# Output weights split two heads earlier and kept in DRAM, the first output projection woven into the last sweeps

## The chip, the cores and the metric

One core of a Trainium2 chip runs one launch of the kernel. The metric is the device time of that core in microseconds (us); the median of the runs of the kernel before is 2640.04 us. Engines are called as the profile calls them: PE (TensorE's matmuls), DVE (VectorE), ACT (ScalarE), POOL (GpSimd) and SP (SyncE, which here only issues DMAs).

## The reference

A block of a transformer-like network on one sequence of 2048 tokens with 1024 features. The part around the change:

```
hx = rmsnorm(x) * (1 + sc1) + sh1                        # modulated by a conditioning vector
heads = 4 HGRN2 heads and 4 retention heads on hx @ w_in # each a scan forward and a scan backward
mix_x = concat(normalised, gated heads)                  # 2048 x 1024
x = x + g1 * (mix_x @ w_out)                             # the output projection
hx2 = rmsnorm(x, norm2_g) * (1 + sc2) + sh2
x = x + g2 * conv_ffn(hx2)                               # up, 3-tap convolution, silu, down
return rmsnorm(x, final_g)
```

All inputs and outputs are 32-bit floats. The scales g1, sc2, sh2 and so on are pieces of silu(c) @ w_mod + b_mod.

## The kernel before

**Numbers.** Big products are made with pairs of 16-bit floats: a block is scaled by a power of two, rounded to f16, and the rest is kept as a second f16. `mm3` (L98) then takes three matmuls, high times high, high times low and low times high, into one accumulator. For the projections of the heads and the feed-forward part a seven-product scheme is used (`unit`, L550); the output projection is plain: 8 blocks k of 128 rows.

**Stages.** `run` (L1830) calls `setup`, `heads`, `out_proj`, `ffn_up` and `ffn_down`. Tokens are in four groups of 512 (`NG`), features in eight blocks of 128 (`KT`).

**Heads.** `heads` (L1027) walks over 32 steps s: head h = 0 to 7 (0 to 3 HGRN2, 4 to 7 retention) and i = 0 to 3 inside it, which takes the groups from the last to the first. A step (`step`, L1002) runs the backward sweep of head h on one group (`ret_sweep1`, L1246: scores times a decay table rA at L1254, transposes, state updates at L1274) and the forward sweep of head h - 1 on group i (`ret_sweep2`, L1281: states at L953, sum at L1286, the sum of squares on ACT at L963, a reciprocal root in small DVE steps at L79 to L90; and `ret_sweep2b`, L1289: scaling and gating at L1293, a transpose otp on PE at L970, a copy m on ACT at L1296 and a store to mixd in DRAM). `weave` (L991) mixes into it, piece by piece, the projection of the next step (`ret_proj`, L1201), which reads the normalised features hx from DRAM through ten tiles (L518, `RING`). Behind step 31 come four steps with only the last head's forward sweeps (L1107); the last head's gates (`ret_gate`, L1191) are the filler of step 31 and of the first two of these.

**Work spread by ticks.** Each step calls `tick` (L325) twice. A tick runs the second half of what it loaded last time, and loads the next n items of a list: weights of the next head (`head_weights`, L709), rows of the modulation (`mod_later`, L294), and in the last head the output weights. `out_weights` (L1311) gives eight items. The load puts 128 rows of w_out into one of two raw tiles (wor, L1323). The second half multiplies by g1 (L1332, DVE), squares and sums (L1334, ACT), adds up over partitions (a small matmul, L124), makes a power of two (`pow2`, L105, five small DVE steps), notes it in so (L1336, L1337), and scales and splits both halves into wo (L1342 on ACT, L1343 on DVE). The wo tiles lie in the slots q and z and stay in SBUF until the projection has used them. For the first block g1 is first spread over the partitions (`broadcast_cols`, L1300, into the slot FG).

**Output projection.** `mixed_pairs(g)` (L1347) finds the group's scale smk (L1361) from the eight values in so and a bound on the gates, then loads mixd block by block (mxf, L1376) and makes pairs mp of it (L1377 on ACT, L1378 on DVE). `out_product(g)` (L1389) takes four tiles of 128 tokens in two halves of 512 columns: 8 x 3 matmuls opp each, then x is added (L1404), squares are summed (L1405), x1 is stored to DRAM and scaled for the second norm (L1408). Its accumulators have the tag pj with three banks. `out_proj` (L1463) puts these together with the second norm (`second_norm_a`, `second_norm_b`), whose tiles y0 to y13 are in a pool that opens only when the head phase's pools are closed.

**What sets the order.** The program's order is the order in which these functions emit. A compile-time scheduler (L1888) then orders each engine's queue by a simulated timeline, so an instruction can be pulled ahead of others that were emitted earlier; each engine, SP too, works off its queue in order. `issue_after(ins)` (used at L312) keeps what is emitted inside it behind the instruction `ins` on its engine; `self.mark` is the last rA or state update of the backward sweep.

## Time and profile before

| | us |
|---|---|
| median of 3 runs | 2640.04 (2639.76 to 2642.2) |
| profiled execution, first to last instruction | 2636.4 |
| what lies around the span, against the median | 3.6 |
| PE busy | 2515.8 (95%) |
| DVE busy | 1887.8 (72%) |
| ACT busy | 1349.2 (51%) |
| POOL busy | 425.2 (16%) |

The profile gives no wall time of its own for the profiled execution, so its span stands in the table beside the median. Times in the profile's answers are counted from the span's first instruction. A line such as `L1332 DVE TENSOR_TENSOR wor<-wor,g1b` names the line of the kernel, the engine, the operation, and the written and read tiles; a bracket such as `[1.67 <-DMA ...]` is the idle time of that engine just before, and what ended it. PEclk is the clock granted to TensorE as a share of the full one. Matmul ends are modelled, so that a busy PE isn't always at its peak.

### The profile page before, as it was taken

How to read it: one execution, taken by the hardware profiler on the slowest of the kernel's cores; microseconds unless marked ns; L12 is line 12 of the kernel's file. 1: busy time of each engine (PE TensorE's matmuls, PEld its weight loads, DVE VectorE, ACT ScalarE, POOL GpSimd, SP SyncE). 2: the span in 40 equal slices, each digit the busy share in tenths (PEclk: the TensorE clock that was granted, in tenths of full speed). 3: DMA queues.
4: the chain of work that ended last, by engine and by line, in shares of the span. 5: the costliest groups of instructions: out<-in, count | busy, mean ns of one | idle time of the engine just before them, and what ended most of it. 6: DMA issues, size and time to landing. Idle time of an engine off the chain costs nothing. (4 is left out here: it accounts for less than half of the span.)

```text
span 2636.4 us, 56190 instructions
## 1 busy us (share of the span) xinstructions
PE 2515.8 (95%) x22763; PEld 1656.9 (63%) x22763; DVE 1887.8 (72%) x4275; ACT 1349.2 (51%) x2877; POOL 425.2 (16%) x409
## 2 busy tenths in 40 slices
PE   6799998999999999988998999999999999999998
PEld 3678887889899999984454444444444444444443
DVE  4888686786878778675558778888888887323656
ACT  5886466564654454453556556565555555211220
POOL 1100000000000000000354334343434433000000
PEclk7999999999999999998999999999999999999999
DMA  8324342441548567555421332333233236544552
GB/s 295 121 95 162 124 142 85 135 152 67 177 161 291 210 210 255 189 198 192 143 81 41 116 106 99 112 107 110 101 116 120 96 113 225 206 165 159 210 206 87
DMA packets 213621, 393.97 MB, mean 149 GB/s; under 512 B 15600, under 2 KB 97748, under 8 KB 208753
## 3 DMA queue, kind: packets, MB, share of 16 engines
q1 hardware_dynamic: 203808, 373.42, 40.8%
q10 hardware_dynamic: 9248, 16.79, 1.9%
q8 instruction: 178, 2.92, 0.5%
q14 instruction: 83, 0.67, 0.1%
q0 software_dynamic: 304, 0.17, 0.0%
HBM read 298.57 MB, written 91.75 MB: 148 GB/s over the span
## 5 line engine op out<-in xcount | busy, mean ns | idle before, releaser
L101 PE MATMUL pa<-feat,w 128*128 128x512 f16 x704 | 265.0, 381 | 7.6 <-ACT ta L592 5.6
L102 PE MATMUL pa<-feat,w 128*128 128x512 f16 x704 | 267.9, 381 | 0.0
L103 PE MATMUL pa<-feat,w 128*128 128x512 f16 x704 | 267.3, 380 | 0.0
L102 PE MATMUL pd<-wd,actl 128*128 128x512 f16 x616 | 233.3, 379 | 0.0
L103 PE MATMUL pd<-wd,actl 128*128 128x512 f16 x616 | 233.3, 379 | 0.0
L101 PE MATMUL pd<-wd,actl 128*128 128x512 f16 x616 | 232.6, 379 | 0.0
L102 PEld LDWEIGHTS <-w 128*128 128x128 f16 x1232 | 120.9, 98 | 150.9 <-issue 13.0
L103 PEld LDWEIGHTS <-w 128*128 128x128 f16 x1232 | 121.0, 98 | 147.0 <-issue 3.2
L101 PEld LDWEIGHTS <-w 128*128 128x128 f16 x1232 | 120.9, 98 | 141.9 <-issue 3.1
L102 PEld LDWEIGHTS <-hx 128*128 128x128 f16 x1824 | 179.4, 98 | 7.7 <-issue 5.9
L1407 POOL TENSOR_TENSOR ssq<-ssq 128x1 f32<-128x1 f32 x16 | 4.7, 292 | 1102.8 <-ACT junk L1405 1102.8
L101 PEld LDWEIGHTS <-hx 128*128 128x128 f16 x1824 | 179.9, 99 | 2.2
L103 PEld LDWEIGHTS <-hx 128*128 128x128 f16 x1824 | 179.6, 99 | 0.9
L1642 ACT ACTIVATE st<-act,modT 128x512 f16<-128x512 f32 x154 | 107.4, 717 | 109.6 <-DVE act L1632 64.1
L1643 DVE SCALAR_TENSOR_TENSOR st<-act,modT,st 128x512 f16<-128x512 f32 x154 | 140.3, 946 | 29.7 <-ACT st L1642 28.8
L101 PE MATMUL pa<-w_vg,hx 128*128 128x128 f16 x800 | 141.8, 219 | 1.1 <-ACT ct L592 0.7
L102 PE MATMUL pa<-w_vg,hx 128*128 128x128 f16 x800 | 141.7, 219 | 0.0
L103 PE MATMUL pa<-w_vg,hx 128*128 128x128 f16 x800 | 141.7, 219 | 0.0
L101 PE MATMUL pc<-feat,w 128*128 128x512 f16 x352 | 134.8, 383 | 2.2 <-ACT feat L1417 1.3
L103 PE MATMUL pc<-feat,w 128*128 128x512 f16 x352 | 135.2, 384 | 0.0
L102 PE MATMUL pc<-feat,w 128*128 128x512 f16 x352 | 135.0, 383 | 0.1
L101 PE MATMUL pa<-hx,w_z 128*128 128x256 f16 x464 | 127.0, 274 | 1.6 <-DVE K L634 1.3
(552 smaller groups left out, 7357.3 us busy)
## 6 DMA issues: line engine op xcount, KB each, us to landing
hx<-hxd SPq DMA_DIRECT2D x212, 512.0 KB, 4.7
actd<-st SPq DMA_DIRECT2D x154, 256.0 KB, 2.0
actl<-actd SPq DMA_DIRECT2D x28, 1024.0 KB, 5.0
wur<-in_w_up_dram SPq DMA_DIRECT2D x44, 512.0 KB, 3.8
raw<-in_w_in_dram SPq DMA_DIRECT2D x36, 512.0 KB, 4.7
wm<-in_w_mod_dram SPq DMA_DIRECT2D x64, 256.0 KB, 3.7
hxd<-hx SPq DMA_DIRECT2D x28, 512.0 KB, 3.9
wdb<-in_w_down_dram SPq DMA_DIRECT2D x44, 256.0 KB, 3.8
```

What stands on the lines that cost most here:

```text
L101: mm(ps, lhs(0), rhs(0), start=start, stop=False, skip_group_check=True)
L102: mm(ps, lhs(0), rhs(1), start=False, stop=False, skip_group_check=True)
L103: mm(ps, lhs(1), rhs(0), start=False, stop=stop, skip_group_check=True)
L1407: nc.gpsimd.tensor_tensor(ssq[:, 0:1], ssq[:, 0:1], ssq[:, 1:2], ALU.add)
L1642: nc.scalar.activation(p[:, 0], v, AF.Copy, scale=s)
L1643: nc.vector.scalar_tensor_tensor(p[:, 1], v, s, p[:, 0], ALU.mult, ALU.subtract)
```

## The change

The output weights' items get three parts (load, square, split) and are spread over ticks from head 6 on, in the gaps behind head 7's weights and the last modulation rows; the list may now run on into head 7, so the loop that empties it ahead of a head's last step is left out for head 6. The multiply by g1 is put behind `self.mark`. Split weights are written to DRAM (wod) and read back, all of them, ahead of head 7's last step (`out_loads`); in between they use only q. `mixed_pairs` is parted into the scales (`mixed_scales`) and the pairs (`mixed_some`), and the output product is made a generator (`out_steps`), one half tile a piece. The four last steps now make group 0's scales and pairs, three half tiles of group 0's product as filler in each of the third and fourth, the second modulation, and group 1's scales and pairs 2 to 7. Group 1 sums its blocks in the order 2 to 7, 0, 1, with pairs 0 and 1 in y0. The fourth x1 tile of group 0 is two half tiles in z instead of y6. The rest of `out_proj` is as it was.

```diff
+        self.wod = [dp.tile([P, 2, 2, 512], F16, name=f"wod{k}") for k in range(KT)]
...
     def tick(self, n=2):
 
-        for comp in self.loaded:
+        later = []
+        for comp, *rest in self.loaded:
             comp()
+            if rest:
+                later.append(rest)
         now, self.todo = self.todo[:n], self.todo[n:]
-        for load, _ in now:
+        for load, *comps in now:
             if load:
                 load()
-        self.loaded = [c for _, c in now]
+            later.append(comps)
+        self.loaded = later
...
+                elif h < 2 * NH - 1:
+                    n = 5
+                    mods = self.mod_later(10) + self.mod_later(11)
+                    outs = self.out_weights()
+                    ticks = [items[:1] + mods[:2], items[1:4] + mods[2:4], items[4:] + mods[4:6], mods[6:] + outs[:1]]
+                    ticks += [[o] for o in outs[1:]]
+                    items = [it for t in ticks for it in t + [none] * (n - len(t))]
                 else:
-                    items = self.out_weights()
-                    self.todo += items[:5]
-                    n = 1
+                    n, items = self.n_tick, []
+                self.todo += items
                 self.n_tick = n
             if i == NG - 1:
-                while self.todo or self.loaded:
-                    self.tick(4)
+                while h != 2 * NH - 2 and (self.todo or self.loaded):
+                    self.tick(self.n_tick)
                 if h == 2 * NH - 1:
-                    self.todo += items[5:]
+                    self.out_loads()
...
+        self.x0 = []
+        first = self.out_steps(0, self.x0)
         for i in range(NG):
-            self.weave(self.step(2 * NH, i, None, None, prev, None), self.ret_gate(NH - 1, i + 2, W, prev) if i < 2 else None, 3, 4)
-            if i == 1:
-                self.mixed_pairs(0)
+            if i == 0:
+                self.mixed_scales(0)
+                self.mixed_some(0, ((0, 1), (2, 3), (4, 5), (6,)))
+                filler, n = self.ret_gate(NH - 1, 2, W, prev), 4
+            elif i == 1:
+                self.mixed_some(0, ((7,),))
+                filler, n = self.ret_gate(NH - 1, 3, W, prev), 4
+            else:
+                if i == 2:
+                    self.mod2 = self.modulation(self.cp, self.kp, self.sv[:, V_N2:V_N2 + 8], self.modT[:, 0, 32:40],
+                                                self.modT[:, 0, 24:32], 1, 4.0)
+                else:
+                    self.mixed_scales(1)
+                    self.mixed_some(1, ((2, 3), (4, 5), (6, 7)))
+                filler, n = islice(first, 3), 3
+            self.weave(self.step(2 * NH, i, None, None, prev, None), filler, 3, n)
+        self.first = first
...
-            def comp():
+            def square():
...
-                w = self.wo[k] = [self.slot_tile([P, 2, 512], F16, "q" if 2 * k + half < 4 else "z", "wo") for half in range(2)]
+                w = raws[k, 1] = self.slot_tile([P, 2, 512], F16, "q", "wos")
                 raw = raws[k]
-                nc.vector.tensor_tensor(raw, raw, self.g1b, ALU.mult)
...
+                with self.tc.issue_after(self.mark.ins):
+                    nc.vector.tensor_tensor(raw, raw, self.g1b, ALU.mult)
+                nc.scalar.activation(w.rearrange("p a n -> p (a n)"), raw, AF.Square, scale=gain(k), accum_out=self.q8[:, k:k + 1])
+
+            def split():
+                raw, w = raws.pop(k), [self.slot_tile([P, 2, 512], F16, "q", "wos"), raws.pop((k, 1))]
+                s, i = self.pow2(self.wp, self.allsum(self.q8[:, k:k + 1]), 1, "w")
...
                     nc.scalar.activation(w[half][:, 0], v, AF.Copy, scale=rk)
                     nc.vector.scalar_tensor_tensor(w[half][:, 1], v, rk, w[half][:, 0], ALU.mult, ALU.subtract)
-            return load, comp
+                    nc.sync.dma_start(self.wod[k][:, half], w[half])
+            return load, square, split
...
+    def out_loads(self):
+
+        for k in range(KT):
+            self.wo[k] = [self.slot_tile([P, 2, 512], F16, "q" if k < 2 else "z", "wo") for half in range(2)]
+            for half in range(2):
+                self.nc.sync.dma_start(self.wo[k][half], self.wod[k][:, half])
...
-            mp = [self.slot_tile([P, 1, 2, G], F16, "z" if k < 2 else "vg", "mp") for k in range(KT)]
+            mp = [None] * 2 + [self.slot_tile([P, 1, 2, G], F16, "vg", "mp") for k in range(2, KT)]
...
+    def mixed_some(self, g, parts):
+
+        nc = self.nc
+        dst, _, smk, mp = self.mixp[g]
+        if mp[0] is None and parts[0][0] == 0:
+            w = self.slot_tile([P, 2, 2, G], F16, "y0", "mp")
+            mp[:2] = w[:, :1], w[:, 1:]
+        for ks in parts:
+            f = self.wp.tile([P, len(ks), G], F32, tag="wr", bufs=WR, name="mxf")
+            for kk, k in enumerate(ks):
                 nc.sync.dma_start(f[:, kk], self.mixd[k][:, g * G:(g + 1) * G])
                 nc.scalar.activation(dst(k)[:, 0], f[:, kk], AF.Copy, scale=smk[:, k:k + 1])
                 nc.vector.scalar_tensor_tensor(dst(k)[:, 1], f[:, kk], smk[:, k:k + 1], dst(k)[:, 0], ALU.mult, ALU.subtract)
...
+    def out_steps(self, g, x1):
+        order = (2, 3, 4, 5, 6, 7, 0, 1) if g == 1 else range(KT)
...
+                for j, k in enumerate(order):
+                    self.mm3(pp, lambda q: mp(k)[:, q, ts], lambda q: wo[k][half][:, q], j == 0, j == KT - 1)
...
     def out_proj(self):
-        self.mod2 = self.modulation(self.cp, self.kp, self.sv[:, V_N2:V_N2 + 8], self.modT[:, 0, 32:40],
-                                    self.modT[:, 0, 24:32], 1, 4.0)
         self.feats = [None, None]
-        x0 = self.out_product(0)
-        self.mixed_pairs(1)
+        x0 = self.x0
+        self.mixed_some(1, ((0, 1),))
+        for _ in self.first:
+            pass
         self.mixed_pairs(2)
```

More of the change, by code (lines that the diff above doesn't have):

```diff
@@ L1 @@
 from contextlib import ExitStack, nullcontext
-from itertools import chain
+from itertools import chain, islice
 import numpy as np
@@ L1371, in mixed_pairs @@
         dst = lambda k: mp[k // n][:, k % n]
-        for k0 in range(0, KT, 2):
-            f = self.wp.tile([P, 2, G], F32, tag="wr", bufs=WR, name="mxf")
-            for kk in range(2):
-                k = k0 + kk
+        self.mixp[g] = dst, io, smk, mp
+    def mixed_some(self, g, parts):
[7 more added lines that the diff above has]
+            for kk, k in enumerate(ks):
                 nc.sync.dma_start(f[:, kk], self.mixd[k][:, g * G:(g + 1) * G])
@@ L1397, in out_product @@
             ts = slice(i * P, (i + 1) * P)
             ssq = self.kp.tile([P, 2], F32, tag="ssq", bufs=2, name="ssq2")
[L1399 to L1400 removed]
+            for half, xh in enumerate(halves):
                 pp = self.ps("pj", [P, 512], "opp")
[L1402 to L1405 removed]
@@ L1411, in modulated, with out_product @@
+            yield
+    def out_product(self, g):
+        x1 = []
+        for _ in self.out_steps(g, x1):
+            pass
+        return x1
     def modulated(self, f, k, xn):
```

67 lines of the change are left out of this document (34 added, 33 removed).

## The prediction, blind

> **What bounds the kernel now.** First the page of the profile, for the whole execution.
>
> ```profile
> span 2636.4 us, 56190 instructions
> ...
> PE 2515.8 (95%) x22763; PEld 1656.9 (63%) x22763; DVE 1887.8 (72%) x4275; ACT 1349.2 (51%) x2877; POOL 425.2 (16%) x409
> ```
>
> TensorE (PE) is busy 95% of the span. The change adds or removes no large matmul, so it can win only where PE stands idle or runs at a lowered clock near the place that is edited. The second view is a table of busy time by stretch of time: from the third step of retention head 2 (the loop's h = 6) to the end of the first group's output projection and the second group's beginning.
>
> ```profile
> core 0: us, PE busy (x) PEld busy (x) DVE busy (x) ACT busy (x) POOL busy (x), PEclk, DMA share, GB/s
> 1030.00:1140.00 110.00, 104.32 (x1201) 98.72 (x1198) 76.21 (x210) 48.31 (x124) 0.00 (x0) 1.00 0.62 212
> 1120.00:1140.00 20.00, 16.13 (x164) 14.45 (x161) 14.33 (x50) 8.36 (x24) 0.00 (x0) 1.00 0.73 251
> 1140.00:1205.00 65.00, 49.28 (x625) 47.28 (x626) 50.20 (x184) 37.62 (x92) 0.00 (x0) 0.87 0.50 167
> 1150.00:1190.00 40.00, 32.17 (x459) 31.61 (x456) 28.93 (x109) 25.93 (x63) 0.00 (x0) 0.96 0.48 171
> 1160.00:1170.00 10.00, 6.66 (x72) 6.41 (x71) 5.46 (x13) 5.48 (x15) 0.00 (x0) 0.84 0.57 217
> 1180.00:1210.00 30.00, 18.13 (x141) 13.98 (x140) 23.58 (x100) 16.35 (x45) 0.00 (x0) 0.77 0.50 140
> 1250.00:1280.00 30.00, 24.93 (x128) 12.39 (x127) 18.04 (x42) 20.16 (x36) 10.60 (x19) 1.00 0.67 206
> ```
>
> Length minus PE busy is the idle time: 3.87 us in 1120 to 1140, 3.34 in 1160 to 1170, 11.87 in 1180 to 1210, 5.07 in 1250 to 1280: 24.15 us. The granted clock adds to it: busy time times the missing share of the clock is 6.66 x 0.16 = 1.1 us in the second and 18.13 x 0.23 = 4.2 us in the third (an average over a stretch, so an estimate). So 29.5 us are there to be won.
>
> Third, who made PE wait (waits of PE, two rows), and the chains behind them (timeline; the bracket is the idle time just before, and what ended it).
>
> ```profile
> PE otp L970 <- DVE ou L1293: 11.9, 2, 6.6
> PE opp L101 <- ACT mp L1377: 3.7, 2, 2.1
> ```
>
> ```profile
> 1126.06 1.23 DVE L1332 TENSOR_TENSOR wor<-wor,g1b 128x1024 f32<-128x1024 f32 x1 [1.67 <-DMA wor<-in_w_out_dram]
> 1127.31 1.15 ACT L1334 ACTIVATE wo<-wor,sv 128x1024 f16<-128x1024 f32 x1 [2.51 <-DVE wor L1332]
> 1130.19 0.27 PE L101 MATMUL pc<-hx,w_z 128*128 128x256 f16 x1 [1.97 <-ACT cb L594]
> ...
> 1163.04 1.22 DVE L1332 TENSOR_TENSOR wor<-wor,g1b 128x1024 f32<-128x1024 f32 x1 [4.29 <-DMA wor<-in_w_out_dram]
> 1166.42 1.84 PE L1265 MATMUL rop<-rV,rA 128*128 128x128 f32 x8 [3.34 <-DVE rA L1254]
> ```
>
> The output-weight preparation hurts PE by standing in line: DVE waits in order for a raw block (wor) still on its way, rA queues behind, and PE waits 3.34 us for rA. At 1126 the same wait goes through ACT's queue.
>
> ```profile
> 1182.45 0.74 DVE L1286 SCALAR_TENSOR_TENSOR ou<-o,qd,ou 128x512 f32<-128x512 f32 x1
> 1192.08 0.48 PE L970 MATMUL otp<-ident,ou 128*128 128x128 f32 x1 [6.57 <-DVE ou L1293]
> 1195.40 1.40 DVE L1343 SCALAR_TENSOR_TENSOR wo<-wor,rk,wo 128x512 f16<-128x512 f32 x2
> 1195.58 0.56 ACT L1296 COPY m<-otp 128x512 f32<-128x512 f32 x1
> 1202.51 0.23 DVE L1361 TENSOR_SCALAR smk<-so,mm 128x8 f32<-128x8 f32 x1
> 1202.77 2.56 ACT L1377 ACTIVATE mp<-mxf,smk 128x512 f16<-128x512 f32 x4 [4.96 <-DVE smk L1361]
> 1203.68 0.63 PE L101 MATMUL opp<-wo,mp 128*128 128x512 f16 x1
> ```
>
> At the head phase's end PE has no filler from 1192.08 - 6.57 = 1185.5 on: the last block is split at 1195.4, only then do all eight scales exist, smk comes at 1202.51, the first pair at 1202.77, and the product starts at 1203.68. In between, PE has only the last head's forward sweeps, whose normalisation on DVE and ACT makes it wait 11.9 us.
>
> **The change part by part.** *Preparation moved forward.* Eight blocks are multiplied, squared and summed, scaled and split, as before.
>
> ```profile
> L1343 DVE SCALAR_TENSOR_TENSOR wo<-wor,rk,wo x16: 739/744/753, 1120.0 to 1196.1; 128x512 f16<-128x512 f32 x16
> ...
> L1334 ACT ACTIVATE wo<-wor,sv x8: 1133/1142/1149, 1111.7 to 1189.5; 128x1024 f16<-128x1024 f32 x8
> ...
> L1332 DVE TENSOR_TENSOR wor<-wor,g1b x4: 1220/1225/1226, 1110.4 to 1135.1; 128x1024 f32<-128x1024 f32 x4
> ```
>
> ```profile
> DVE wor L1332 <- DMA wor<-in_w_out_dram: 10.8, 5, 4.3
> ```
>
> On DVE a block costs 1.22 + 2 x 0.744 us and eight small steps of 0.23 us at most (smk's row; I take 0.18): 4.2 us, or 34 us for eight. Four of the multiplies lay before 1140, so about 17 us of this are new in 1030 to 1140. By the new list of ticks the first square is emitted in the third step of head 6 and the last split in the third step of head 7, which these two rows date (rA opens a step):
>
> ```profile
> 1030.32 0.68 DVE L1254 TENSOR_TENSOR rA<-rsc,Dm 128x512 f32<-128x512 f32 x1
> ...
> 1137.00 0.68 DVE L1254 TENSOR_TENSOR rA<-rsc,Dm 128x512 f32<-128x512 f32 x1
> ```
>
> So DVE goes from 76 to about 93 us of 110 there, and from 50 to 33 of 65 after it. ACT, with a 1.14 us square and two casts a block, has more room in both. This work lies beside PE's projections; if the cover fails, what is due next is rA and the evacuations, and PE pays. What goes is the head-of-line wait: 3.87 + 3.34 + 1.1 = 8.3 us at most. But a block's load is still emitted one tick ahead of its multiply and waits for the split of the block two before it. New is that the multiply is held behind the step's mark on DVE, so that rA or the state updates go first, and that ACT's cast comes a tick after its square. Between 0 and 8.3 I take 5, nearer the top, because the two quoted chains cannot form at these places any more.
>
> *Scales early, projection as filler.* The eight scales are ready some 50 us before the first group's last head is. smk and the pairs of k = 0 to 6 then wait for nothing of the weights, and the product's 24 matmuls a half tile can fill the two idle times at the sweeps; three accumulators (pj has three banks) take work before k = 7 must be there. k = 7 still needs the last head's first sweep, from L1286 at 1182.45 to its m at 1195.58; without the block's work queued in DVE and ACT in between it should come 4 to 5 us sooner. The most is 11.87 + 4.2 = 16.1 us; the least, if PE stands at k = 7, about 2. I take 12. What is late next is k = 7's trip through memory, priced among the rivals.
>
> *Second group.* The 5.07 us after 1250 are mostly the 3.7 us of opp <- mp above, for group 1's pairs and their scales. Six of its eight pairs are now made in the last sweep and used first; pairs 0 and 1 wait for y0, space that the head phase frees late. Between 0 and 5.1 I take 3. The fourth x1 tile in z instead of y6 lets group 0 end without that space; it costs one more load, store and scaling, beside other work. The second modulation moves from after the sweeps into the third sweep: some twenty small steps of at most 0.23 us, under 5 us of DVE time in its emptier stretch; I give it nothing, and 2 us if that cover fails.
>
> *Weights through memory.* Sixteen stores and sixteen loads of 262 KB: 4.2 MB each way. All stand on SP's queue. A store waits there for its split, and behind it wait the hx loads for PE; before, a raw block's load waited there in the same manner:
>
> ```profile
> SPq L1323 <- DVE wo L1343: 11.2, 4, 5.9
> ```
>
> The nearest price is thus 2.8 us of SP a wait (5.9 at most); hx has a ring of ten tiles as cover, and PE's list of waits above has no row for hx. The reload is emitted ahead of head 7's fourth step, so between that step's predecessor at 1137.00 and PE's wait for its rA at 1166.42, say at 1150, and stands ahead of the mixd loads. In 1150 to 1190 the core moved 171 GB/s; at the 251 of 1120 to 1140 another 80 GB/s x 40 us = 3.2 MB fit, against 4.2 of reload and 2.1 of mixd, less the raw blocks no longer loaded there. The excess of up to 3.1 MB is 12 us of transfer at worst, though the product can begin on the first blocks. For stores, SP and the reload together I take 3 us, from 0 to 12.
>
> The Trainium skill has a rule that speaks against the reload (DMA: Bandwidth & Descriptors, section "Anatomy of one DMA", stated for the gpsimd path): a transfer costs about 2.0 us plus its bytes at 436 GB/s. Taken one after another, sixteen pieces are then 42 us, and a reload begun at 1150 lands at 1192, 7 us after PE runs dry; by that rule the sum would be 7 us less, 2630. The 251 GB/s row speaks against taking it serially, since one such piece in 2.6 us would be only 100 GB/s.
>
> **Sum.** 5 + 12 + 3 - 3 = 17 us. The profiled execution spans 2636.4 us, 3.6 less than the median of 2640.04, and I take what lies around the span as unchanged: 2619.4 in the span, 2623.0 as a median.
>
> **Rivals.** *The start stays pinned to k = 7.* PE works in order; if the matmul with k = 7 of the first half tile is queued ahead of the next half tile's, PE stands at it. The trip is, by these rows,
>
> ```profile
> mixd<-m ACTq DMA_DIRECT2D x9, 256.0 KB, 5.2
> mxf<-mixd SPq DMA_DIRECT2D x8, 256.0 KB, 4.8
> ```
>
> 10 us from m to the pair's input, or 1205.6 from today's m; with m 4 to 5 us sooner, about 1201, near today's 1203.68. Then 2 of the 16.1 us are won: 5 + 2 + 3 - 3 = 7, 2633. For it speaks that k = 7 is the last in each sum, against it the free accumulators.
>
> *The reload is late.* By the shares above up to 12 us, less the 4 to 5 us by which the first product can wait for k = 7 anyway; the likely loss is 7 us, 2630. For it speaks the share above, against it that 1140 to 1205 ran at only 167 GB/s with the DMA engines half idle.
>
> *Slower: SP's queue becomes the bound.* Eight splits, each with stores that SP waits for in line, in the stretch where hx loads feed every projection. It decides when PE loses over 20 / 8 = 2.5 us a block (20 being the gains before the 3 us charged). With 3.5 us, between the 2.8 and the 5.9 of the SP row, the loss is 28 against 20: 8 us slower, 2648. For it speaks DVE at 85%, which makes splits late; against it that the hx loads wait for freed tiles anyway.
>
> **How the numbers follow.** About 0.2%, 5.3 us, is what a measurement of this kernel can tell from no change. Forecast 0.62, pinned 0.14, late reload 0.10, slower 0.09, and 0.05 that gains and new waits cancel. Faster by over 0.2%: all of the forecast but a tail, and most of the two milder rivals, 0.81; same 0.10; slower 0.09. The range goes from the whole 29.5 us (2610) to 2637, where a pinned start meets low ends: 0 for the weights' waits or for the second group's pairs instead of 5 and 3 us. The slower case and the cancelling one are outside.
>
> **What would show it.** Right: no DVE wait for wor over 1 us after 1140, wo multiplies from about 1050, opp's first matmul near 1180 and ahead of the last head's second sweep, PE over 28 of 30 us and clock 1.00 in that stretch. Wrong: PE waits for hx or for rA in heads 6 and 7, SP waits for the split over 2.5 us a block, or opp standing on mp or wo for several us.

## The result, and the profile after

The changed kernel takes 2622.4 us (median of 4 runs, 2617.45 to 2625.79), the kernel before, beside it, 2640.54 (4 runs, 2639.76 to 2642.2): a ratio of 0.9927, 95% interval 0.9915 to 0.9939. The forecast was 2623.0. One of the five runs of e7_reload_twice, below, took 4237.06 us at a granted clock of 0.564 and is left out of its median. The profiled execution of the changed kernel is the fastest of its four, 2617.45 us with a span of 2615.7, so the two profiles lie 20.7 us apart (2636.4 - 2615.7) where the medians lie 18.1 apart.

The page of the profile after, its head:

```profile
span 2615.7 us, 56265 instructions
...
PE 2509.6 (96%) x22763; PEld 1653.6 (63%) x22763; DVE 1887.9 (72%) x4276; ACT 1348.6 (52%) x2877; POOL 424.9 (16%) x409
```

PE runs the same 22763 matmuls in 6.2 us less busy time (2515.8 - 2509.6): that is clock. Added up over the span in windows of 2.5 us, busy time times the missing share of the granted clock falls from 32.1 to 24.5 us (an estimate); only 3.2 us of this fall lie between 1030 and 1280, where the change works. The other 14.5 us of the span are idle time that went. The table of busy time by stretch of time, for the stretches that the prediction read, shows where (columns as there):

```profile
core 0: us, PE busy (x) PEld busy (x) DVE busy (x) ACT busy (x) POOL busy (x), PEclk, DMA share, GB/s
1030.00:1140.00 110.00, 101.37 (x1147) 95.38 (x1146) 85.64 (x250) 55.98 (x136) 0.00 (x0) 0.98 0.75 251
1120.00:1140.00 20.00, 17.65 (x207) 16.45 (x206) 17.53 (x54) 9.62 (x28) 0.00 (x0) 1.00 0.90 304
1140.00:1205.00 65.00, 63.49 (x729) 52.84 (x727) 45.38 (x159) 32.69 (x84) 0.00 (x0) 1.00 0.72 260
1160.00:1170.00 10.00, 10.00 (x138) 9.96 (x136) 5.50 (x27) 5.53 (x12) 0.00 (x0) 1.00 1.04 408
1180.00:1210.00 30.00, 28.49 (x190) 15.88 (x188) 14.37 (x56) 10.43 (x27) 0.19 (x1) 1.00 0.38 122
1250.00:1280.00 30.00, 30.00 (x152) 15.03 (x151) 13.31 (x17) 14.62 (x31) 13.25 (x28) 1.00 0.54 182
```

The reader is to see three things. In the three last stretches PE is full or nearly so (10.00 of 10, 28.49 of 30, 30.00 of 30) at clock 1.00, where before it was 6.66, 18.13 and 24.93 at 0.84, 0.77 and 1.00. The first row went the other way: 101.37 busy in 110 instead of 104.32. And the DMA engines, at 408 GB/s in 1160 to 1170, show a busy share of 1.04 while PE loses nothing.

The waits of PE from 1030 to 1280, longest sums first, show what is left:

```profile
PE rob L1298 <- DVE Kt L1300: 2.3, 2, 1.6
PE otp L975 <- DVE ou L1319: 1.8, 1, 1.8
PE allsum L124 <- ACT w_g L743: 1.8, 1, 1.8
PE opp L101 <- ACT mp L1427: 1.5, 1, 1.5
PE pa L101 <- DVE p2i L115: 0.9, 1, 0.9
PE allsum L124 <- ACT wos L1360: 0.6, 1, 0.6
```

The wait for w_g stands in the trace of before too (1.81 us at 1043.80). The two waits of 6.6 and 3.3 us for otp and rop are gone, and so are those of opp but for one. New are the rows for Kt, p2i and wos: all of them lie between 1060 and 1110, where the trace of before shows no wait of PE. Here is the stretch around them, first before, then after:

```profile
1050.00:1120.00 70.00, 70.00 (x810) 66.92 (x810) 47.84 (x127) 29.96 (x78) 0.00 (x0) 1.00 0.57 193
...
1050.00:1120.00 70.00, 65.59 (x737) 61.73 (x738) 55.07 (x162) 36.59 (x85) 0.00 (x0) 1.00 0.75 251
```

The next fence shows the timeline of the changed kernel at four places: block 0's multiply, two multiplies of late raw blocks, and the tail.

```profile
1059.82 1.23 DVE L1359 TENSOR_TENSOR wor<-wor,g1b 128x1024 f32<-128x1024 f32 x1 [2.09 <-ACT g1b L1335]
...
1062.52 0.49 PE L1298 MATMUL rob<-Kt,K 128*128 128x128 f32 x2 [1.61 <-DVE Kt L1300]
...
1090.26 1.23 DVE L1359 TENSOR_TENSOR wor<-wor,g1b 128x1024 f32<-128x1024 f32 x1 [1.93 <-DMA wor<-in_w_out_dram]
...
1091.66 0.15 DVE L115 TENSOR_SCALAR p2i<-p2t 128x1 f32<-128x1 f32 x1
1091.80 0.22 PE L101 MATMUL pa<-w_v,hc 128*128 128x128 f16 x1 [0.85 <-DVE p2i L115]
...
1126.48 1.23 DVE L1359 TENSOR_TENSOR wor<-wor,g1b 128x1024 f32<-128x1024 f32 x1 [2.02 <-DMA wor<-in_w_out_dram]
...
1129.41 1.14 DVE L1319 SCALAR_TENSOR_TENSOR ou<-ou,rs_y,gate 128x128 f32<-128x128 f32 x4
1129.82 0.33 PE L975 MATMUL otp<-ident,ou 128*128 128x128 f32 x1 [1.83 <-DVE ou L1319]
...
1175.37 0.22 DVE L1403 TENSOR_SCALAR smk<-so,mm 128x8 f32<-128x8 f32 x1
1176.02 2.54 ACT L1427 ACTIVATE mp<-mxf,smk 128x512 f16<-128x512 f32 x4
1190.08 0.59 ACT L1322 COPY m<-otp 128x512 f32<-128x512 f32 x1 [3.37 <-PE otp L975]
1199.22 0.72 ACT L1427 ACTIVATE mp<-mxf,smk 128x512 f16<-128x512 f32 x1 [5.97 <-DMA mxf<-mixd]
...
1199.99 0.39 PE L101 MATMUL opp<-wo,mp 128*128 128x512 f16 x1 [1.51 <-ACT mp L1427]
```

At 1059.82 DVE has waited 2.09 us for the spread gate g1b, and PE pays 1.61 us for Kt behind it. At 1090.26 and 1126.48 the multiply at the head of DVE's queue has waited for a raw block still on its way; the steps behind it are late (p2i, the normalisation of L1319), and PE pays 0.85 and 1.83 us. In the tail, smk is there at 1175.37 instead of 1202.51, the pairs are made from 1176, and ACT copies the tile m of k = 7 at 1190.08 instead of 1195.58; its pair follows 9.1 us later, at 1199.22, and PE, which has had other matmuls until 1198.48, waits 1.51 us for it. By the grouped row of L101, which holds the output products of all four groups (4 x 8 half tiles x 8 blocks = 256), the product starts at 1182.1 and its last matmul at 1367.8, 22.8 us earlier than before:

```profile
L101 PE MATMUL opp<-wo,mp x256: 376/379/390, 1182.1 to 1367.8; 128*128 128x512 f16 x128
```

### The profile page after: what moved, and what is told of

The parts are those of the page before. It is cut to its first block, busy times and chain, and to the rows that moved or that the text cites. A ratio compares the mean times of both kernels' runs of the same rounds, so it can differ in the third digit from the quotient of the medians.

```text
span 2615.7 us, 56265 instructions
## 1 busy us (share of the span) xinstructions
PE 2509.6 (96%) x22763; PEld 1653.6 (63%) x22763; DVE 1887.9 (72%) x4276; ACT 1348.6 (52%) x2877; POOL 424.9 (16%) x409
## 5 line engine op out<-in xcount | busy, mean ns | idle before, releaser
L101 PE MATMUL pa<-feat,w 128*128 128x512 f16 x704 | 265.5, 381 | 9.8 <-ACT ta L597 6.8
L101 PE MATMUL pd<-wd,actl 128*128 128x512 f16 x616 | 232.6, 379 | 0.0
L101 PEld LDWEIGHTS <-w 128*128 128x128 f16 x1232 | 120.7, 98 | 142.1 <-issue 2.4
L101 PEld LDWEIGHTS <-hx 128*128 128x128 f16 x1824 | 179.8, 99 | 2.1
L101 PE MATMUL pa<-w_vg,hx 128*128 128x128 f16 x800 | 143.0, 220 | 1.0 <-ACT ct L597 0.7
L101 PE MATMUL pc<-feat,w 128*128 128x512 f16 x352 | 133.6, 380 | 2.8 <-ACT tb L597 1.5
L101 PE MATMUL pa<-hx,w_z 128*128 128x256 f16 x464 | 127.1, 274 | 1.6 <-DVE K L639 1.2
```

The costliest lines, as they stand in the source:

```text
L101: mm(ps, lhs(0), rhs(0), start=start, stop=False, skip_group_check=True)
```

## The experiments

**The measure.** The profiles differ by some us ahead of any edit that matters here: PE's wait for w_g, which every kernel has, ends between 1041.25 and 1049.78 in the fourteen profiles. So beside the times the table has the "stretch", from the end of that wait to the last start of opp at L101 (before: 1390.6 - 1043.80 = 346.8; after: 1367.8 - 1041.91 = 325.9), and PE's idle time (length less PE busy) in 1050 to 1150, 1150 to 1240 and 1240 to 1380. The column "clock" is an estimate of what PE loses in the stretch to a lowered clock: busy time times the missing share of the granted clock, in windows of 2.5 us. Idle time and clock taken off, 314.5 to 317.4 us of the stretch are left in every kernel, 313.2 and 313.6 in the two that prepare one block. So differences of the stretch are idle time and clock, but for up to 3 us. Each kernel has one profile; how far the stretch varies between executions of one kernel isn't shown. The experiments ran in four groups on different chips, each beside the kernel before, with medians of 2640.32, 2641.7, 2640.04 and 2638.06; each ratio goes by the kernel before on the same chip.

| kernel | median us | ratio to before, 95% | idle us in the three stretches | clock us | stretch us |
|---|---|---|---|---|---|
| before | 2640.54 | | 4.38, 15.34, 5.06 | 5.1 | 346.8 |
| after | 2622.4 | 0.9927 (0.9915 to 0.9939) | 6.76, 1.51, 0.00 | 1.7 | 325.9 |
| e1_sweeps_as_before | 2627.58 | 0.9950 (0.9937 to 0.9962) | 6.61, 3.78, 4.88 | 4.6 | 337.3 |
| e2_weights_as_before | 2631.9 | 0.9970 (0.9958 to 0.9982) | 4.44, 11.77, 0.91 | 5.0 | 338.5 |
| e3_no_mark | 2617.58 | 0.9913 (0.9900 to 0.9927) | 8.82, 0.00, 0.00 | 1.4 | 325.9 |
| e4_one_block | 2614.14 | 0.9904 (0.9889 to 0.9920) | 7.08, 0.09, 0.00 | 2.9 | 323.3 |
| e5_k7_direct | 2618.18 | 0.9916 (0.9899 to 0.9934) | 6.24, 0.15, 0.30 | 1.7 | 324.4 |
| e6_second_late | 2623.97 | 0.9939 (0.9923 to 0.9956) | 6.58, 3.95, 2.27 | 1.4 | 331.5 |
| e7_reload_twice | 2618.61 | 0.9915 (0.9896 to 0.9934) | 8.15, 0.00, 0.01 | 1.6 | 325.7 |
| e8_reload_held | 2621.53 | 0.9926 (0.9909 to 0.9944) | 7.34, 1.25, 0.25 | 1.6 | 327.2 |
| e9_one_block_held | 2609.03 | 0.9886 (0.9870 to 0.9901) | 1.78, 0.10, 0.20 | 0.0 | 315.7 |
| e10_k7_no_mark | 2617.15 | 0.9924 (0.9910 to 0.9937) | 9.00, 0.00, 0.69 | 1.6 | 328.2 |
| e11_gate_apart | 2609.68 | 0.9891 (0.9878 to 0.9905) | 5.01, 0.02, 0.07 | 0.0 | 321.2 |
| e12_raw_in_ring | 2613.7 | 0.9900 (0.9884 to 0.9917) | 5.64, 0.00, 0.00 | 1.7 | 321.8 |

**Each half alone.** The first run keeps the early weights, their stores and reloads, and puts the tail back: the first group's scales and pairs behind the second of the last four sweeps, the product behind the fourth. The second modulation, the second group's order and the x1 tile go back with it; the diff shows the edit in part.

```diff
-        first = self.out_steps(0, self.x0)
         for i in range(NG):
...
-            self.weave(self.step(2 * NH, i, None, None, prev, None), filler, 3, n)
+            self.weave(self.step(2 * NH, i, None, None, prev, None), self.ret_gate(NH - 1, i + 2, W, prev) if i < 2 else None, 3, 4)
+            if i == 1:
+                self.mixed_pairs(0)
```

> The output weights are prepared two heads early and kept in DRAM as in the changed kernel, but the sweeps at the end, the pairs and the output projection are emitted in the order of the kernel before. Theory A (what counts is that the eight scales and the weights exist early; the scheduler pulls the product into the idle times by itself, as it did before at 1203.68): the product's first matmul comes near 1185 again, and the time is 2621 to 2627 us, at most 5 us over the changed kernel. Theory B (what counts is the weaving): the pairs of group 0 come only behind the second forward sweep, the product's first matmul stays near 1200, and the time is 2632 to 2638 us.

The second keeps the new tail and puts the weights' preparation back into the last head, without the trip through memory. The first group's scales and pairs come one sweep later than in the changed kernel.

```diff
-                    outs = self.out_weights()
-                    ticks = [items[:1] + mods[:2], items[1:4] + mods[2:4], items[4:] + mods[4:6], mods[6:] + outs[:1]]
...
                 else:
-                    n, items = self.n_tick, []
+                    items = self.out_weights()
+                    self.todo += items[:5]
+                    n = 1
```

> The other half alone: the output weights are prepared in head 7 and behind it, into tiles that stay, as in the kernel before; the sweeps at the end have the new order, with the scales of group 0 behind the first forward sweep. Theory A: the start stays pinned to the eighth block, first matmul of the product at 1200 to 1206, DVE waits for raw blocks of some 10 us in all, and the time is 2636 to 2643 us, less only what the earlier pairs of group 1 bring (3 us). Theory B: 2622 to 2630 us.

Each came out between its two forecasts, 2627.6 (2621 to 2627, 2632 to 2638) and 2631.9 (2636 to 2643, 2622 to 2630): neither half is the cause alone. In the stretch they win 9.5 and 8.3 us of 20.9; the remaining 3.1 need both. The waits of PE, first of the first run in 1180 to 1260, then of the second in 1130 to 1285, show what each half lacks:

```profile
PE opp L101 <- ACT mp L1411: 5.1, 4, 2.2
PE otp L975 <- DVE ou L1303: 2.9, 1, 2.9
```

```profile
PE otp L971 <- DVE ou L1309: 7.0, 2, 6.5
PE rop L1281 <- DVE rA L1270: 3.0, 1, 3.0
PE pc L101 <- ACT cb L595: 2.2, 1, 2.2
```

With early weights alone the wait for otp falls from its 6.6 us to 2.9 though PE has no new filler, and DVE's timeline there has no step of a block between those of the normalisation any more; only the waits for the second group's pairs stay. With the new tail alone the filler is emitted but can't run: smk comes at 1199.7, behind the last block, the product's first matmul at 1201.2, and the wait for otp is 6.5 us as before.

**The mark.** The multiply isn't held behind rA and the state updates.

```diff
-                with self.tc.issue_after(self.mark.ins):
-                    nc.vector.tensor_tensor(raw, raw, self.g1b, ALU.mult)
+                nc.vector.tensor_tensor(raw, raw, self.g1b, ALU.mult)
```

> As the changed kernel, but the multiply by g1 is not held behind the last rA or state update. If the mark is what keeps the blocks' waits for their loads from stopping rA and the state updates, DVE's waits for raw blocks rise from 7.4 us to 10 or more, PE loses 3 to 6 us more between 1040 and 1160, and the time is 2625 to 2629 us. If the mark does next to nothing, the time stays within 2 us of the changed kernel's 2622.

Measured 2617.6 us, not slower and below both forecasts, and the same stretch, 325.9. But the same is a sum of two: idle time in 1050 to 1150 is 2.1 us higher (8.82 against 6.76), and the 1.5 us at k = 7 aren't there; the product's first matmul starts only at 1191.4. The waits of PE in 1050 to 1140 name rA, which the changed kernel's list doesn't have, and DVE's list for 1030 to 1180 the raw blocks as before:

```profile
PE rop L1291 <- DVE rA L1280: 2.4, 1, 2.4
PE allsum L124 <- ACT m L1322: 2.2, 1, 2.2
```

```profile
DVE wor L1358 <- DMA wor<-in_w_out_dram: 7.4, 5, 2.1
```

So the mark does put rA first; it doesn't make DVE wait less for raw blocks (7.4 us with it in 4 waits, 7.4 without it in 5).

**One block.** Only the first of the eight blocks is loaded, multiplied, squared, split and stored; the other scales are copies of its, and all sixteen reloads read it. The product is then that of one block used eight times.

```diff
             def load():
+                if k:
+                    return
...
             def square():
+                if k:
+                    return
...
             def split():
+                if k:
+                    for j in range(2):
+                        nc.vector.tensor_copy(self.so[:, j, k:k + 1], self.so[:, j, 0:1])
+                    return
...
-                self.nc.sync.dma_start(self.wo[k][half], self.wod[k][:, half])
+                self.nc.sync.dma_start(self.wo[k][half], self.wod[0][:, half])
```

> As the changed kernel, but only the first block of w_out is loaded, scaled, split and stored; the other seven are left out, and all eight reloads read the first block's pairs, so the projection is computed with wrong weights. If the preparation is what costs PE the new waits between 1040 and 1135 (6.3 us of idle time there, against 1.8 before), most of these go and the time is 2615 to 2619 us. If they come from the reload or the crowded DMA queues, which stay, the idle time there stays at 4 us or more and the time within 2 us of 2622.

Measured 2614.1 us, below both forecasts; the stretch is only 2.6 us shorter than the changed kernel's, about what the seven missing sums of 0.38 us took on PE (313.2 us of work left instead of 315.9). The idle time of 1050 to 1150 stayed at 7.08, as the second forecast had it, but it is another one: 5.46 us in one piece. Reloads that wait for one block's stores only are drawn forward to 1077, eleven of them by 1089, and the timeline shows ACT behind them and PE behind ACT:

```profile
1092.66 0.37 ACT L686 ACTIVATE rckv<-pa,dqk 128x128 f32<-128x128 f32 x1 [6.87 <-DMA wo<-wod]
...
1093.08 0.27 PE L101 MATMUL pb<-hc,w_z 128*128 128x128 f16 x1 [5.46 <-ACT rckv L686]
```

From 1082 to 1090 the DMA engines move 405 GB/s. What ACT waited for is the profile's inference; that the early reloads are behind it is shown below, where they are held and the wait is gone. This run alone couldn't tell the steps' cost from the reloads'. The next ones do.

**Four changes to the changed kernel: k = 7, second group, reload twice, reload held.**

```diff
+        if h == NH - 1 and g == 0:
+            self.m7 = m
+        else:
             nc.scalar.dma_start(self.mixd[4 + h][:, g * G:(g + 1) * G], m)
...
+            direct = g == 0 and ks == (7,)
+            if direct:
+                f = self.m7.rearrange("p (a t) -> p a t", a=1)
```

> The pair of k = 7 of the first group is made from the tile m in SBUF, without the trip through memory (one store and one load of 256 KB less); all else as in the changed kernel. In its profile the first matmul with k = 7 was waited for 1.51 us, ending at 1199.99, the only idle time over 0.4 us between 1140 and 1380. Theory A (the start was still pinned to k = 7, a little): this wait goes, 1.5 us less, 2620 to 2621, and the product's first dense run starts some 8 us earlier. Theory B (PE in that stretch is full anyway, work only changes places): 2622, the same, and the wait comes back at the forward sweeps (otp or o2 waiting for DVE).

The wait at k = 7 is gone (0.15 us of idle time in 1150 to 1240, from 1.51) and nothing took its place: the stretch is 1.5 us shorter, as theory A had it. The median of 2618.2 is lower than forecast, but the ratios' intervals overlap (0.9899 to 0.9934 against 0.9915 to 0.9939), so that the time by itself doesn't decide; nor did the product's first matmul come 8 us earlier, but at 1180.8 instead of 1182.1.

```diff
-                else:
-                    self.mixed_scales(1)
-                    self.mixed_some(1, ((2, 3), (4, 5), (6, 7)))
...
+        self.mixed_scales(1)
+        self.mixed_some(1, ((2, 3), (4, 5), (6, 7)))
+        self.mixed_some(1, ((0, 1),))
```

> The second group's scales and its pairs 2 to 7 are made behind the last sweep and the rest of the first group's product, as before the change; all else as in the changed kernel. Theory A (the early pairs are what removed the idle time of 5.07 us at the second group's beginning): PE waits for mp or smk there again, 3 to 5 us more, 2625 to 2627. Theory B (the removed idle time came from the scales of the weights being ready and DVE being empty by then): 2622 to 2623, the same, with no idle time over 1 us between 1240 and 1290.

Theory A by the trace: the stretch is 5.6 us longer, 4.6 of it idle time, and the timeline has PE waiting for the late pairs, twice:

```profile
1235.56 0.39 PE L101 MATMUL opp<-wo,mp 128*128 128x512 f16 x1 [1.72 <-ACT mp L1424]
...
1247.32 0.61 PE L101 MATMUL opp<-wo,mp 128*128 128x512 f16 x1 [2.26 <-ACT mp L1424]
```

The 0.61 us of the second, against 0.39, goes with a lowered clock behind the wait (0.50 from 1248.05 to 1250.55). The median rose by 1.6 us only, to a value between the two forecasts; the trace, not the time, carries this verdict.

```diff
             for half in range(2):
-                self.nc.sync.dma_start(self.wo[k][half], self.wod[k][:, half])
+                for _ in range(2):
+                    self.nc.sync.dma_start(self.wo[k][half], self.wod[k][:, half])
```

> Each of the sixteen pieces of reloaded weights is loaded twice into the same tile, 4.2 MB more on SP's queue and the DMA engines; all else as in the changed kernel. Theory A (the reload has slack: it is hidden behind PE work, since the last piece landed by about 1170 and the product begins at 1182): within 2 us of the changed kernel, 2621 to 2624. Theory B (the reload crowds the loads that feed the last projections and is part of the 5.9 us of new waits between 1030 and 1120; or it makes the first product wait): 5 to 12 us more, 2627 to 2634, with waits of PE for hx, rckv or wo.

4.2 MB more, and neither the time (2618.6, below the forecast 2621 to 2624) nor the stretch (325.7) grew: theory A. PE has no idle time at all from 1150 to 1240. One wait did grow, from 1.83 to 3.26 us, at otp behind DVE's wait for a raw block, and 1.6 us of lowered clock follow it. The changed kernel loses as much clock elsewhere, behind the wait for w_g, so that a cost of some 2 us isn't excluded.

```diff
-                    nc.sync.dma_start(self.wod[k][:, half], w[half])
+                    self.stored = nc.sync.dma_start(self.wod[k][:, half], w[half])
...
+                with self.tc.issue_after(self.stored.ins):
+                    self.nc.sync.dma_start(self.wo[k][half], self.wod[k][:, half])
```

> All sixteen reloads are held on SP's queue behind the last store of a split, so none of them stands between the stores and the head's loads from 1096 on; all else as in the changed kernel. Theory A (the new waits of 1030 to 1120 come from the preparation's work on DVE and ACT): they stay, 2622, and the reload, now from about 1153 on, either fits before the product or adds up to 5 us where the product waits for wo. Theory B (they come from reloads drawn forward among the head's own loads): idle time over 0.4 us between 1060 and 1120 goes, 3 to 5 us less, 2617 to 2619, if the product doesn't wait for wo.

Theory A: the waits of 1050 to 1150 stay (7.34 us). The reload, all of it late, shows how short it is. The group of the reloads' issues (count, duration in ns, first and last start), and the row of issues (KB each, median us to landing):

```profile
L1383 SPq DMA_DIRECT2D wo<-wod x16: 319/406/977, 1156.4 to 1168.0; - x16
```

```profile
wo<-wod SPq DMA_DIRECT2D x16, 256.0 KB, 5.9
```

Sixteen pieces are issued in 11.6 us and have landed some 6 us after the last issue, before the product starts at 1186.2. In the same profile the largest wait of PE follows from a raw block that is late, with no reload in sight:

```profile
1128.44 1.23 DVE L1359 TENSOR_TENSOR wor<-wor,g1b 128x1024 f32<-128x1024 f32 x1 [3.91 <-DMA wor<-in_w_out_dram]
...
1131.78 0.43 PE L975 MATMUL otp<-ident,ou 128*128 128x128 f32 x1 [3.72 <-DVE ou L1319]
```

**One block, reloads held.** As the run with one block, with the sixteen reloads behind the last load of hx that is issued ahead of them; again the product is that of one block.

```diff
-            self.nc.sync.dma_start(X[m], self.hxd[g][m])
+            self.stored = self.nc.sync.dma_start(X[m], self.hxd[g][m])
...
+                with self.tc.issue_after(self.stored.ins):
+                    self.nc.sync.dma_start(self.wo[k][half], self.wod[0][:, half])
```

> Only the first of the eight weight blocks is multiplied, squared, split and stored, and all sixteen reloads read it (so the product is that of one block used eight times); the reloads are held on SP's queue behind the last load of hx that is issued ahead of them. The run with one block and free reloads kept 7.07 us of idle time between 1050 and 1110, of which 5.46 us in one piece behind sixteen reloads that came early. Theory A (the new waits of 1050 to 1140 have two sources, the seven later blocks' steps in DVE's, ACT's and PE's queues, and reloads among the head's own transfers): with both gone, idle time between 1050 and 1140 falls to about 1.6 us, the wait of the first block's multiply for the broadcast gate, and the time to 2612 or less. Theory B (the waits come from the modulation that is moved forward in heads 6 and 7, or from anything else): 4 us or more stay there, 2615 to 2618.

Theory A. The row of the table by stretches for 1050 to 1150:

```profile
1050.00:1150.00 100.00, 98.22 (x1142) 93.85 (x1140) 71.26 (x207) 42.92 (x117) 0.00 (x0) 1.00 0.73 244
```

1.78 us of idle time, of which 1.61 is the wait for Kt behind block 0's multiply. The moved modulation, which this kernel keeps, brings no wait of PE that the list shows. The seven blocks' preparation is thus the source of the new waits, and DVE is busy 71.26 us here and 80.28 in the changed kernel. Their steps, their loads and their stores were taken out together, so that this run doesn't part them. The stretch is 10.2 us shorter: 6.2 are idle time, 1.7 the clock behind the wait for w_g, which isn't charged to the change below, and some 2 the seven blocks' sums on PE, which a real projection needs. So about 6 us could still be had here.

**Better versions.** First, k = 7 direct and no mark, the two edits shown above together.

> The two changes that each gave nothing worse together: k = 7 of the first group straight from SBUF, and no mark that holds the weights' multiply. Theory A (they act in different places, 1200 and 1060 to 1140): 2616 to 2619, 0 to 2 us under k = 7 alone, with no idle time over 0.6 us between 1140 and 1380. Theory B (the mark matters once the rest is full): 2 us or more above k = 7 alone, 2620 to 2623, with waits of PE for rA or Kt between 1050 and 1140.

2617.2 us, with 9.00 us of idle time in 1050 to 1150 and a stretch 3.8 us longer than with k = 7 direct alone, 2.8 of it idle time in 1050 to 1150. The time lies in theory A's interval, the trace has theory B's waits (rop for rA 1.3 us, allsum for m 3.2). By the trace the mark is worth 2 to 3 us; by the times that isn't resolved.

Second, k = 7 direct with the mark, and block 0's broadcast gate one tick ahead of its multiply.

```diff
-            def square():
+            def gate():
                 if k == 0:
                     self.g1b = self.slot_tile([P, D], F32, "FG", "g1b")
...
-            return load, square, split
+            return (load, square, split) if k else (load, gate, square, split)
...
-                    ticks += [[o] for o in outs[1:]]
+                    ticks += [[none]] + [[o] for o in outs[1:]]
```

> k = 7 from SBUF, and the broadcast of the gate g1b is emitted one tick ahead of the first block's multiply (all later blocks one tick later), so that DVE's multiply finds g1b made. In the changed kernel DVE waits 2.09 us for g1b at 1059.82, and PE 1.61 us for Kt behind it, the same 1.61 in every version with early weights. Theory A (the multiply that waits in DVE's queue causes PE's wait): the 1.61 us go, and nothing takes their place, 2616 to 2617. Theory B (the wait belongs to the four matmuls and copies of the broadcast or to the state chain, or the later blocks now press on the tail): the idle time between 1050 and 1140 stays at 6 to 7 us or new waits come after 1140, 2618 to 2621.

2609.7 us (2607.03 to 2615.26), 6 us under the lower forecast, ratio 0.9891 (0.9878 to 0.9905): faster than both kernels, with an interval clear of the changed kernel's. The 1.61 us are gone; two shorter waits came beside the place (0.68 for ACT's m and 1.12 for ACT's Kt), so theory A holds in part: 5.01 us of idle time in 1050 to 1150 instead of 6.24, and a stretch 3.2 us shorter than with k = 7 alone. Of these 3.2 only 1.6 are idle time; 1.7 are the lowered clock behind the wait for w_g, which k = 7 alone has and this kernel hasn't, though the wait is the same 1.81 us. Its profile is of its slowest run, and the rest of the difference in the medians isn't located.

Third, the same with the raw blocks in hx's ring of ten tiles.

```diff
-                raws[k] = self.wp.tile([P, D], F32, tag="wr", bufs=WR, name="wor")
+                raws[k] = self.slot_tile([P, D], F32, "hx", "wor")
```

> As the kernel with k = 7 from SBUF and the gate apart (2609.7), but the raw weight blocks are loaded into tiles of hx's ring of ten instead of the two raw buffers, so that a block's load doesn't wait for the split of the block two before it. In that kernel DVE waits for raw blocks 6.9 us in 5 waits, and in the changed kernel such a wait of 2.02 us stands ahead of PE's 1.83 us for otp at 1129.82. Theory A (the two raw buffers make the loads late, and the multiply that waits at the head of DVE's queue passes it on to PE): DVE's waits for wor fall below 2 us in all, and PE's idle time between 1050 and 1180 from 5.0 to 3 us or less, 2607 to 2609. Theory B (the ring was full of use: each raw block takes an hx tile for two ticks, and hx comes later): PE waits for hx, 2612 to 2620.

Both theories at once. DVE's waits for raw blocks are gone altogether, and PE's for otp behind them; instead PE waits once for hx:

```profile
1135.39 0.28 PE L101 MATMUL pa<-hx,w_z 128*128 128x256 f16 x1 [3.59 <-DMA hx<-hxd]
```

2613.7 us, the stretch 321.8 against 321.2, and 5.64 us of idle time from 1050 to 1180 where theory A had 3 or less: the wait was moved, not won.

## Why the prediction was right, point by point

**The sum.** 17 us were forecast, 18.1 measured between the medians and 20.7 between the profiles. The terms, against the idle time and clock of the same stretches:

| term | forecast | measured in the profile |
|---|---|---|
| weights' waits, of 8.3 | 5 | 6.0 (2.35 us of idle time left, in 1120 to 1140) |
| scales early, product as filler, of 16.1 | 12 | 14.6 (1.51 left) |
| second group, of 5.1 | 3 | 5.1 (none left) |
| stores, SP, reload | -3 | -4.4 (idle time in 1050 to 1120, 70 us long, PE busy 65.59), and not by these |

That gives 21.3; from it goes the lowered clock behind the wait for w_g, 0.66 in 1041.91 to 1046.91, 5.00 x 0.34 = 1.7 us (an estimate). Of seven other kernels whose profiles have the same wait of 1.81 us, the kernel before among them, two show a lowered clock behind it and five don't, so it isn't charged to the change. 19.6 of the 20.7 us are so accounted for; in 1030 to 1280 PE's idle time and clock loss together fall by the same 19.6 (16.5 and 3.2). Right in kind, then, with the two gains of the tail sized too low by 2.6 and 2.1 us, the weights' by 1.0, and the charge too low by 1.4. That the gain between the medians came within 1.1 us of the forecast is in part luck: errors of both signs met, and the spread of the four runs, 8 us, is larger.

**Scales early, projection as filler.** smk was expected well ahead of the last head, m of k = 7 four to five us earlier, and its pair at 1201: they came at 1175.37, 1190.08 (5.5 earlier) and 1199.22. The eight scales were complete at 1149.5, some 40 us ahead of that m and not 50. What the prediction put too little weight on is that clearing the tail's queues does most of it. With early weights and the old tail the idle time of 1150 to 1240 is 3.78 us, from 15.34; weaving the product in takes off 2.3 more there, and it can do so only with early scales (11.77 are left without them). The rival that the start stays pinned to k = 7 was true of 1.5 us and not of 14: PE had enough to do until 1198.48, and opp's first matmul came 17 us ahead of the pair.

**The second group.** The step held, and was worth its whole 5.1 us; made late again, the pairs cost 5.6 us of stretch.

**The step that failed: "the two quoted chains cannot form at these places any more".** The one through rA doesn't: the changed kernel's list has no wait for rA, and without the mark 2.4 and 1.3 us of it are back. The other does. DVE's list of waits for 1030 to 1280 after has

```profile
DVE wor L1359 <- DMA wor<-in_w_out_dram: 7.4, 4, 2.4
...
DVE wor L1359 <- ACT g1b L1335: 2.1, 1, 2.1
```

against 10.8 us before. A raw block's load still waits for the split of the block two before it: block 3's was issued at 1085.38, 0.4 us after block 1's split had ended (1084.23 + 0.75), and DVE's multiply, waiting for it, began 4.9 us later, at 1090.26. And the multiply still stands first in DVE's queue; the mark chooses what goes ahead of it, not what is held up behind it. The prediction said of the load that nothing had changed, and then didn't draw the conclusion. "No DVE wait for wor over 1 us after 1140" was right, but only because the last block is multiplied at 1137.1: the waits had moved to 1090 to 1130 with the blocks (and the one for g1b to 1060). DVE was also expected at 93 us in 1030 to 1140 and had 85.64, since the last splits end at 1152, later than the ticks were dated.

**The charge of 3 us: near in size, for another cause.** It was put on the stores, SP and the reload. SP's stores do wait for DVE, more than expected (which of DVE's steps released them is inferred):

```profile
SPq L1373 <- DVE wos L1372: 11.5, 6, 4.3
...
SPq L1373 <- DVE rs_t L88: 10.6, 2, 10.3
...
SPq L1373 <- DVE rs_y L89: 4.4, 3, 3.5
...
SPq L1373 <- DVE Sf L958: 2.9, 1, 2.9
```

These four rows are 29.4 us for eight blocks, 3.7 a block, where the slower rival was to decide at 2.5. PE nevertheless has no wait for hx in the changed kernel: the threshold took SP's wait for PE's, and the ring of ten stood between them. Where raw blocks take tiles of that ring, PE does wait for hx, 3.59 us. The larger waits that PE pays between 1050 and 1140 follow from the blocks' steps in the in-order queue of DVE: 1.61 us behind the wait for g1b, 0.85 and 1.83 behind waits for raw blocks; 0.6 are a block's sum in PE's own queue (allsum behind wos). With one block and held reloads 1.78 us of idle time are left in 1050 to 1150. The store in front of a raw block's load on SP's queue adds little: the load of 1085.38 was issued 0.4 us after its tile was free.

**The late reload.** It was dated to 1150; the scheduler drew it forward to 1096.7, where it runs between the stores. Doubled, it lengthened neither the time nor the stretch; held until 1156, the sixteen pieces take 11.6 us to issue and about 18 until they have landed, ahead of the product. By the rule of the Trainium skill weighed in the prediction (DMA: Bandwidth & Descriptors, section "Anatomy of one DMA"), taken one after another, it would have been an estimate of 42 us; the pieces overlap, and the 18 us decide. A reload can hurt where it crowds other transfers, though: with eleven pieces drawn forward by 1089, as with one block, it cost 5.46 us.

**Not settled.** The 1.7 us of lowered clock behind the wait for w_g, which come and go between versions; the rest of the clock's gain, which lies outside 1030 to 1280; which of the blocks' steps, loads and stores costs how much; and why the best version's median lies lower than its stretch explains.

## What to carry to other kernels

Take preparation out of the stage whose dependent chain is longest, even if its steps then cost more elsewhere: here 4.4 us of new waits in a full stage bought 26 us of old ones. Look for what stands first in an in-order queue and waits for a transfer, since ordering it later doesn't help what is behind it; emit its operand a stage ahead (here the gate, whose wait went), and if you feed it from another ring, look at who else needs that ring. And when a wait of a DMA queue is to be priced, ask for the wait of the engine that it feeds, because a ring of buffers can hide 3.7 us a block altogether and then fail at once when it is used for something else.

## What the runs showed of the hardware

The DMA engines moved 408 GB/s in 1160 to 1170 of the changed kernel with PE busy 10.00 of 10 us; at 405 GB/s in 1082 to 1090 of the run with one block PE was busy 5.62 of 8 us. The rate alone doesn't say whether PE loses. Stores and reloads of the split weights are issued in turn on one queue, with 3.7 and 6.4 us from issue to landing (medians of sixteen pieces of 256 KB). The same wait of 1.81 us for w_g is followed by 5 us at a granted clock of 0.66 in three of eight profiles and at 1.00 in five. And the wait for w_g ends up to 8.5 us apart between profiles (1041.25 and 1049.78, in the versions with k = 7 direct and with the gate apart), which is more than several of the effects told here; a stretch that is measured inside one profile leaves this out.
